# One core, a hybrid decoder layer: in its attention the loads of the next two heads are issued behind the second of eight query blocks instead of the fourth

## The chip, the core and the metric

The kernel runs on one core of a Trainium2 chip. It computes one decoder layer for 1024 tokens of width 1024 in float32. The metric is the device time of one execution in microseconds (us). Engines are called as in the profile: PE multiplies matrices, DVE works on vectors, ACT does activation functions, POOL simple work, and SP issues DMAs. SP's queue (SPq) is in order: a DMA whose semaphore wait is not met holds back every DMA behind it.

## The reference

Only the attention half of the layer matters here. Each query keeps the 256 keys with the highest indexer score; the kernel does that with an additive mask per query block, so that every query block of 128 rows meets all its causal keys. `setup_inputs` draws the inputs at random.

```python
def dsa_attention(q, k, v, iq, ik, iw):        # 8 heads of 64, 1024 tokens
    def block(i):                              # 128 queries
        ...
        _, idx = lax.top_k(score, topk)
        valid = idx <= qpos[None, :, None]
        ks = k[bidx, idx]
        vs = v[bidx, idx]
        s = jnp.einsum('bqhd,bqkhd->bhqk', qb, ks).astype(jnp.float32) * scale
        s = jnp.where(valid[:, None], s, -jnp.inf)
        p = jax.nn.softmax(s, axis=-1).astype(v.dtype)
        return jnp.einsum('bhqk,bqkhd->bqhd', p, vs)

def reference(...):
    proj = x @ w_in[l]                         # q, k, v, indexer and HGRN2 columns
    ...
    mix = jnp.concatenate([att, hgo], axis=-1) @ w_o[l]
    x = layer_norm(ALPHA * x + mix, ln1_g[l], ln1_b[l])
    h = jnp.square(jax.nn.relu(x @ w_up[l])) @ w_down[l]
    x = layer_norm(ALPHA * x + h, ln2_g[l], ln2_b[l])
```

## The kernel before

The kernel goes through the layer in stages: the input projection with the indexer's scores, the search for the 256th score and the HGRN2 heads beside it (to about 464 us), the attention (464 to 622 us), the output product with `w_o` and the first layer norm, the up product, the down product. Earlier stages have written the turned queries to DRAM as `qd`, the turned keys as `kd` and the values as `vd`; the additive masks lie on the core as `score` and `causal`.

The attention takes the eight heads in four pairs, hp = 0 to 3. For a pair `fetch` (line 658) issues seven DMAs on SP: two for the queries `qs` and four for the keys (two for each of the two `ks` tiles, one tile a head), each of 512 KB, and one for the values `va`, 512 KB too. In the rows below pair 1 and pair 3 have tiles of their own for queries and values (`qs1`, `va1`), which some views print as `qs` and `va` also; pairs 0 and 2 share one tile each. The `ks` tiles come from a ring of five buffers. Within `fetch` the first key DMA is told to wait for an instruction of ACT (`behind`, line 669): the last exp that had been written down before the call.

For each of the eight query blocks t of a pair, `scores(hp, t)` (line 674) makes on PE the products of the queries with the keys of both heads (lines 691 and 692, a bank of four at a time), moves them on DVE through the mask with a running maximum (line 693), negates the maximum on POOL (line 695), and takes the exp on ACT (line 697). `turn` (line 701) then transposes the exps on PE (line 710) into one of two banks, which DVE and ACT copy out as `pt` (lines 719 and 717); `gather` (line 722) multiplies them with the values two turns later (lines 733 to 738). `normalise` (line 748) has four products at line 751. The query blocks stand in the order t = 0, 1, 4, 5, 2, 3, 6, 7, and the turns of one group of two blocks stand behind the scores of the next group. So the scores of the next pair's blocks 0 and 1 come while blocks 6 and 7 of the pair before are still to be turned and gathered; this place is called the switch to a pair below.

The loop of line 770 walks through that plan and counts the calls of `scores` in `ns`. Pair 1 is fetched at ns = 4 of pair 0, in any case. Pairs 2 and 3 are fetched behind the block whose number is `FT`:

```python
            if (ns == 4 or ns > 8 and u[0] == FT) and hp < 3:
                fetch(hp + 1, pairs[hp]["last"])
```

FT is 5, which is the fourth block in the order above. Tiles and semaphore waits are set by the framework, which also simulates the program to set the order on each engine; where it puts the DMAs on SP is shown with the change.

Of the kernel before, what the change touches and what calls it, by code (L numbers as in the profile page):

```python
# [42 lines left out]
def layer(ctx, tc, x, w_in, w_o, lb_logits, hg_norm_g, ln1_g, ln1_b, w_up, w_down, ln2_g, ln2_b,  # L43
# [608 lines left out]
    bp = es_b.enter_context(tc.tile_pool(name="bp", bufs=1, reuse_waits="tile"))  # L652
    scale = HD ** -0.5
    PB = 5, 4
    PT, LAG, FT = 8, 2, 5
    pairs, probs, parts = {}, {}, {}

    def fetch(hp, after=None):
# [507 lines left out]
```

## Time and profile before

| what | value |
|---|---|
| median of 3 runs | 1389.93 us (1387.81 to 1395.92) |
| the profiled execution, its own time | 1392.06 us |
| its span, first to last instruction | 1390.3 us |
| PE busy | 1313.0 us, 94% of the span |
| DVE, ACT, POOL busy | 70%, 43%, 27% |
| mean granted clock of PE | 0.977 of full speed |
| PE idle for keys, line 691 | 7.4 us in three waits |

The profile is of one execution. The 1.8 us between its time and its span lie outside the instructions. A busy engine is not by that the one that sets the end; the chain of work that ended last and the idle time in front of PE's instructions say where time is lost. Everything that the change touches lies between 505 and 612 us.

### The profile page before, as it was taken

The page shows a single profiled execution, that of the slowest core. Times are in us where ns is not written, and L with a number is a line of the kernel's source. Part 1 is how long each engine was busy: PE and PEld are TensorE (multiplying, and loading weights), DVE is VectorE, ACT ScalarE, POOL GpSimd, SP SyncE. Part 2 cuts the span into 40 slices and gives each one's busy share as a digit, 9 for nine tenths or more (in the row PEclk, how much of TensorE's full clock was granted, in tenths as well). Part 3 has the DMA queues.
Part 4 walks back from the last instruction along what each step waited for, and adds up shares of the span by engine and source line. Part 5 has one row for each costly group of instructions (what it writes and reads, how often), then busy time and mean ns, then how long its engine had stood idle before and what let it go on. Part 6 is the DMA issues. An engine that isn't in the chain of part 4 may idle for free.

```text
span 1390.3 us, 20796 instructions
## 1 busy us (share of the span) xinstructions
PE 1313.0 (94%) x7961; PEld 1068.8 (77%) x7961; DVE 968.8 (70%) x1821; ACT 595.2 (43%) x1038; POOL 371.1 (27%) x344
## 2 busy tenths in 40 slices
PE   8999799789899999999998999999998899999996
PEld 8877678677679956667887888888886688888875
DVE  4556999999993445552278755666536999887568
ACT  3433346555422545552135555555545343333131
POOL 3433312534524201122472000000003432341016
PEclk9999999999999999999999999999999999999998
DMA  5333322101103364306422444444466554442123
GB/s 218 108 101 104 99 59 61 47 18 33 47 32 92 88 125 107 76 16 187 131 106 83 160 159 167 135 145 144 159 212 234 197 186 157 156 159 91 57 96 121
DMA packets 96948, 162.50 MB, mean 117 GB/s; under 512 B 5832, under 2 KB 41040, under 8 KB 96720
## 3 DMA queue, kind: packets, MB, share of 16 engines
q1 hardware_dynamic: 81584, 133.37, 31.0%
q10 hardware_dynamic: 15264, 27.79, 5.7%
q8 instruction: 63, 1.03, 0.3%
q14 instruction: 37, 0.30, 0.1%
HBM read 114.48 MB, written 46.66 MB: 116 GB/s over the span
## 4 chain that ended last, share of the span: by engine, by line
PE 63%; DVE 18%; DMA 8%; POOL 4%; issue 3%; ACT 3%; SPq 1%; POOLq 0%; DVEq 0%; ACTq 0%
PE ps L124 18%; PE ps L123 18%; PE ps L125 18%; DVE junk L313 5%; PE ps L736 3%; DMA ks<-kd 2%; DMA wraw<-in_w_in_dram 2%; PE ps L710 2%; DMA qd<-rparts 1%; DVE hgk L500 1%; POOL tn L911 1%; PE ps L691 1%; DVE hgq L499 1%; POOL acc L837 1%; DMA kd<-rparts 1%
## 5 line engine op out<-in xcount | busy, mean ns | idle before, releaser
L123 PE MATMUL ps<-tw,sh 128*128 128x512 f32 x392 | 153.9, 396 | 8.9 <-ACT tw L88 5.1
L123 PE MATMUL ps<-w,xt 128*128 128x512 f32 (+2 forms) x448 | 157.4, 356 | 2.3 <-ACT hgf L443 1.1
L125 PE MATMUL ps<-w,xt 128*128 128x512 f32 (+2 forms) x448 | 158.4, 355 | 0.0
L124 PE MATMUL ps<-w,xt 128*128 128x512 f32 (+2 forms) x448 | 157.9, 354 | 0.0
L124 PE MATMUL ps<-tw,sh 128*128 128x512 f32 x392 | 154.0, 393 | 1.0 <-DVE tw L89 1.0
L125 PE MATMUL ps<-tw,sh 128*128 128x512 f32 x392 | 152.5, 392 | 1.4 <-DVE sh L89 1.4
L89 POOL TENSOR_TENSOR w<-wraw,w 128x1024 fp32r<-128x1024 f32 (+2 forms) x46 | 95.5, 2086 | 117.8 <-ACT w L88 114.4
L1052 POOL TENSOR_TENSOR tt<-rb,rb 128x1536 f32<-128x1536 f32 (+1 forms) x5 | 19.4, 3873 | 392.9 <-DVE tw L89 327.0
L1074 DVE TENSOR_TENSOR acc<-acc,ps 128x512 f32<-128x512 f32 x140 | 92.1, 679 | 35.8 <-PE ps L125 35.6
L88 ACT ACTIVATE sh<-rs 128x1536 fp32r<-128x1536 f32 (+1 forms) x35 | 49.1, 1403 | 151.2 <-PE ps L125 141.1
L123 PE MATMUL ps<-xt,w 128*128 128x512 f32 x256 | 103.5, 404 | 0.0
L124 PE MATMUL ps<-xt,w 128*128 128x512 f32 x256 | 102.5, 400 | 0.0
L125 PE MATMUL ps<-xt,w 128*128 128x512 f32 x256 | 102.5, 401 | 0.0
L313 DVE TENSOR_SCALAR_CACHE_REDUCE junk<-score,cand 128x384 uint8<-128x384 f32 (+1 forms) x124 | 100.4, 810 | 2.7
L124 PE MATMUL ps<-xt,wq 128*128 128x512 f32 x256 | 99.9, 390 | 0.0
L123 PE MATMUL ps<-xt,wq 128*128 128x512 f32 x256 | 99.7, 389 | 0.0
L125 PE MATMUL ps<-xt,wq 128*128 128x512 f32 x256 | 99.5, 390 | 0.0
L345 ACT ACTIVATE sjunk<-score,scand 128x896 int8<-128x896 f32 (+1 forms) x62 | 67.9, 1095 | 67.7 <-DVE scand L355 49.8
L123 PEld LDWEIGHTS ps<-w,xt 128*128 128x128 f32 x448 | 85.7, 192 | 14.3 <-ACT hgf L443 1.5
L123 PEld LDWEIGHTS ps<-tw,sh 128*128 128x128 f32 x392 | 74.7, 191 | 25.8 <-ACT tw L88 5.5
L124 PEld LDWEIGHTS ps<-w,xt 128*128 128x128 f32 x448 | 85.5, 191 | 11.3 <-issue 0.8
L125 PEld LDWEIGHTS ps<-w,xt 128*128 128x128 f32 x448 | 85.6, 191 | 10.1
(240 smaller groups left out, 3081.4 us busy)
## 6 DMA issues: line engine op xcount, KB each, us to landing
hs<-h ACTq DMA_DIRECT2D x98, 256.0 KB
rs<-hs SPq DMA_DIRECT2D x28, 768.0 KB
wr<-in_w_up_dram SPq DMA_DIRECT2D x16, 1024.0 KB
rb<-in_w_down_dram SPq DMA_DIRECT2D x16, 768.0 KB
wraw<-in_w_in_dram SPq DMA_DIRECT2D x20, 512.0 KB
ks<-kd SPq DMA_DIRECT2D x16, 512.0 KB
xn<-in_x_dram SPq DMA_DIRECT2D x8, 512.0 KB
kd<-rparts SPq DMA_DIRECT2D x16, 256.0 KB
```

What stands on the lines that cost most here:

```text
L88: first = ACT.activation(hi, src, AF.Copy)
L89: (eng or DVE).tensor_tensor(lo, src, hi.bitcast(F32), op=OP.subtract)
L123: PE.matmul(ps, ah, bh, start=first, stop=False, **kw)
L124: PE.matmul(ps, ah, bl, start=False, stop=False, **kw)
L125: PE.matmul(ps, al, bh, start=False, stop=last, **kw)
L313: DVE.tensor_scalar(junk[:, :wide[j]], score[j], at, 0.0, op0=op, op1=OP.add, accum_out=res)
L345: ACT.activation(sjunk[:, :wide[NB + j]], score[NB + j], AF.Sign, bias=0.0 if bias is None else bias[:, j:j + 1], scale=1.0, accum_out=cnt ...
L499: DVE.tensor_tensor(qv[:, :, 1, :], qv[:, :, 1, :], t2[:, :, 0:1].to_broadcast([P, nb, m]), op=OP.mult)
L710: PE.transpose(tp[:, g % 2, i], probs[hp, 2 * m + i][hh][:, g * P:(g + 1) * P], ident)
L736: PE.matmul(o[sl, i:i + 2], lhs, pt[hh][:, g], start=c == 0 and g == 0, stop=c == m)
L1052: POOL.tensor_tensor(t1, b12, b11, op=OP.subtract)
L1074: DVE.tensor_tensor(acc[t][:, gs], acc[t][:, gs], ps, op=OP.add)
```

## The change

One number in line 655 is changed.

```diff
-    PT, LAG, FT = 8, 2, 5
+    PT, LAG, FT = 8, 2, 1
```

With it `fetch` for pairs 2 and 3 is called behind block t = 1 of the pair before, the second block, and the exp that its first key DMA waits for is that of block 1 instead of that of block 5. `fetch` itself, what it loads, the tiles and their number are the same. Pairs 0 and 1 are fetched as before.

On SP, the piece from the queries of pair 2 to the first weights of the next stage is this (`qs`, `va` without a number are the tiles of pair 2, those with a number the tiles of pair 3; x4 is four rows alike):

```order
 L49 DMA qs<-qd 64x2x1024 x2
+L49 DMA ks<-kd 64x2x1024 x4
 L49 DMA va<-vd 128x8x128
+L49 DMA qs_5806<-qd 64x2x1024 x2
 L49 DMA ks<-kd 64x2x1024 x4
-L49 DMA qs_5898<-qd 64x2x1024 x2
-L49 DMA va_5907<-vd 128x8x128
-L49 DMA ks<-kd 64x2x1024 x4
+L49 DMA va_5815<-vd 128x8x128
 L49 DMA wraw<-in_w_o_dram 128x2x512 x5
```

In both pairs the four key DMAs have moved ahead of the value DMA of their own pair; the queries still come first.

What the DMAs of pair 2 wait for on SP, with the change (DMAHW names are earlier DMAs, Activation is ACT):

```order
L49 DMA qs<-qd 64x2x1024 [waits DMAHW0_49,PE_49]
L49 DMA qs<-qd 64x2x1024 [waits DMAHW1_49]
L49 DMA ks<-kd 64x2x1024 [waits DMAHW2_49,Activation_49]
L49 DMA ks<-kd 64x2x1024 [waits DMAHW3_49]
L49 DMA ks<-kd 64x2x1024 [waits DMAHW4_49]
L49 DMA ks<-kd 64x2x1024 [waits DMAHW5_49]
L49 DMA va<-vd 128x8x128 [waits DMAHW6_49,PE_49]
```

The wait for ACT is now that for the exp of block 1 of pair 1, and the value DMA, which waits for PE to be done with the values of pair 0 in the same tile, no longer stands in front of the keys.

On PE, at the switch to pair 2, the rows with the change stand in the same order as before, and only the names of the DMAs that they wait for are others:

```order
 L691 MATMUL ps<-ks,qs_5200 128x512 [waits DVE_49]
 L692 MATMUL ps<-ks,qs_5200 128x512
-L691 MATMUL ps<-ks,qs 128x128 [waits DMAHW3_49,DMAHW1_49,DMAHW4_49,DMAHW0_49,DVE_49]
+L691 MATMUL ps<-ks,qs 128x128 [waits DMAHW2_49,DMAHW1_49,DMAHW3_49,DMAHW0_49,DVE_49]
 L692 MATMUL ps<-ks,qs 128x128
 L710 MATMUL ps<-ident,prs 128x128 [waits Activation_49]
 L710 MATMUL ps<-ident,prs 128x128 x3
-L691 MATMUL ps<-ks,qs 128x128 [waits DMAHW6_49,DMAHW5_49,DVE_49]
+L691 MATMUL ps<-ks,qs 128x128 [waits DMAHW5_49,DMAHW4_49,DVE_49]
 L692 MATMUL ps<-ks,qs 128x128
 L691 MATMUL ps<-ks,qs 128x256 [waits DVE_49]
```

Nothing has moved there; the two rows that wait for DMAs are the scores of block 0 with the keys of the pair's first and second head. On DVE, ACT and POOL no row is different.

## Rows read from the trace of the kernel before

**Rows 1.** The page: span; busy time by engine; the ended-last chain's shares by line.

```profile
span 1390.3 us, 20796 instructions
...
PE 1313.0 (94%) x7961; PEld 1068.8 (77%) x7961; DVE 968.8 (70%) x1821; ACT 595.2 (43%) x1038; POOL 371.1 (27%) x344
...
PE ps L124 18%; PE ps L123 18%; PE ps L125 18%; DVE junk L313 5%; PE ps L736 3%; DMA ks<-kd 2%; DMA wraw<-in_w_in_dram 2%; PE ps L710 2%; DMA qd<-rparts 1%; DVE hgk L500 1%; POOL tn L911 1%; PE ps L691 1%; DVE hgq L499 1%; POOL acc L837 1%; DMA kd<-rparts 1%
```

**Rows 2.** Waits, 455 to 645 us: waiter, releaser: us in total, times, longest.

```profile
PE ps L691 <- DMA ks<-kd: 7.4, 3, 3.3
```

**Rows 3.** PE's timeline, three switches: start, us, instruction, count [idle before <-releaser].

```profile
505.17 0.44 PE L691 MATMUL ps<-ks,qs 128*128 128x128 f32 x1 [3.31 <-DMA ks<-kd]
...
538.15 0.62 PE L710 MATMUL ps<-ident,prs 128*128 128x128 f32 x4
541.37 0.30 PE L691 MATMUL ps<-ks,qs 128*128 128x128 f32 x1 [2.60 <-DMA ks<-kd]
...
576.56 0.62 PE L710 MATMUL ps<-ident,prs 128*128 128x128 f32 x4
578.62 0.30 PE L691 MATMUL ps<-ks,qs 128*128 128x128 f32 x1 [1.44 <-DMA ks<-kd]
```

**Rows 4.** PE's timeline, the same work behind the second and third switch.

```profile
544.23 3.28 PE L736 MATMUL ps<-pt,va 128*64 128x256 f32 x21
...
550.82 0.60 PE L710 MATMUL ps<-ident,pr 128*128 128x128 f32 x4
...
580.64 2.59 PE L736 MATMUL ps<-pt,va 128*64 128x256 f32 x21
...
586.53 0.60 PE L710 MATMUL ps<-ident,pr 128*128 128x128 f32 x4
```

**Rows 5.** Stretches: us, busy PE PEld DVE ACT POOL; PEclk, DMA share, GB/s.

```profile
508.00:510.00 2.00, 2.00 (x7) 0.86 (x8) 0.98 (x7) 1.28 (x5) 0.21 (x1) 0.50 0.00 0
...
512.00:526.00 14.00, 14.00 (x88) 8.77 (x86) 6.50 (x21) 4.56 (x10) 1.04 (x3) 1.00 0.00 0
...
542.00:544.00 2.00, 2.00 (x9) 0.96 (x7) 0.54 (x4) 2.00 (x4) 1.08 (x2) 0.56 1.05 217
544.00:546.00 2.00, 2.00 (x12) 1.10 (x12) 1.03 (x4) 0.29 (x2) 0.38 (x1) 0.58 0.13 25
...
580.00:582.00 2.00, 2.00 (x19) 1.24 (x19) 1.05 (x4) 2.00 (x4) 1.51 (x2) 1.00 0.00 0
```

**Rows 6.** SP's timeline: start, us of issuing, DMA, count.

```profile
526.10 0.37 SPq L49 DMA_DIRECT2D va<-vd  x1
527.99 2.52 SPq L49 DMA_DIRECT2D ks<-kd  x4
...
566.41 2.52 SPq L49 DMA_DIRECT2D ks<-kd  x4
```

**Rows 7.** ACT's timeline: ends of the exps of three blocks.

```profile
510.18 0.19 ACT L697 ACTIVATION_READ_ACCUMULATOR prs<-prs,nm 128x1 f32 x1
...
544.10 0.19 ACT L697 ACTIVATION_READ_ACCUMULATOR pr<-pr,nm 128x1 f32 x1
...
550.60 0.19 ACT L697 ACTIVATION_READ_ACCUMULATOR prs<-prs,nm 128x1 f32 x1
```

**Rows 8.** PE's timeline: the two line-751 groups of pair 1 and of pair 3.

```profile
522.99 1.05 PE L751 MATMUL ps<-ident,wide 128*128 128x128 f32 x8
...
536.15 1.08 PE L751 MATMUL ps<-ident,wide 128*128 128x128 f32 x8
...
597.10 1.05 PE L751 MATMUL ps<-ident,wide 128*128 128x128 f32 x8
...
610.27 1.08 PE L751 MATMUL ps<-ident,wide 128*128 128x128 f32 x8
```

**Rows 9.** PE's timeline behind pair 3, where no next pair follows.

```profile
612.10 0.65 PE L710 MATMUL ps<-ident,prs 128*128 128x128 f32 x4
613.23 0.55 PE L710 MATMUL ps<-ident,prs 128*128 128x128 f32 x3 [0.47 <-DVE pt L719]
```

## The prediction

> **What bounds the kernel now.** I read the page first. PE is busy for 94% of the span, and in the chain of work that ended last the products at lines 123 to 125 come first; but one transfer of the attention stands in it too, the keys `ks` from `kd`, with 2% of the span [rows 1]. That chain has PE in the attention nearly all the time, so what counts there is where PE stands idle. The list of waits between 455 and 645 us names it: PE, at line 691, waited three times for the key transfer, 7.4 us in all, at most 3.3 [rows 2]. PE's own timeline puts the three pauses at the switches to pairs 1, 2 and 3: 3.31 us before 505.17, 2.60 us before 541.37, and 1.44 us before 578.62; the last two come right behind four transposes [rows 3]. The pause at pair 1 belongs to a fetch that the change leaves alone. So the change can work on 2.60 + 1.44 = 4.04 us of pauses, and on what they drag along.
>
> They do drag something along. From the end of the second pause at 541.37 to the transposes at 550.82 PE took 9.45 us; the same instructions behind the third switch, 578.62 to 586.53, took 7.91 us, and 21 products inside took 3.28 us against 2.59 [rows 3, 4]. The granted clock tells why: 0.56 and 0.58 in the two stretches from 542 to 546, where it was part of the time at the lower of its two levels (1.2 instead of 2.4 GHz), and 1.00 behind the third switch [rows 5]. PE had been idle for 2.60 us before the fall and for 1.44 us where none came. So the second pause cost 1.54 us more than its own length.
>
> **The change part by part.** What it moves is one call of `fetch` in pair 1 and one in pair 2, seven DMAs each, all on SP; it adds and removes no instruction, and no row moves on PE, DVE, ACT or POOL.
>
> The keys of pair 2. The first of the four key DMAs left SP at 527.99 [rows 6], and PE went on with the second head's keys at 541.37, 13.38 us later. With the change they wait for the exp of block 1, which ended at 510.18 + 0.19 = 510.37 [rows 7]; the queries stand ahead of them and wait only for pair 0's scores. The DMA engines moved nothing from 512 to 526 [rows 5], so there is room. With the old 13.38 us the keys lie on the core at 523.75. PE wants them when its four transposes before the pause end, 538.15 + 0.62 = 538.77 [rows 3]: 15.0 us to spare. The pause of 2.60 goes, and with it the reason that I see for the low clock: 2.60 + 1.54 = 4.14 us.
>
> The keys of pair 3. They left at 566.41 and PE went on at 578.62, 12.21 us later [rows 3, 6]. With the change they wait for the exp of block 1 of pair 2, which ended at 550.79 [rows 7] and will end 4.14 earlier, at 546.65; by the longer of the two transfers they are there at 560.03, and PE wants them at 577.18 - 4.14 = 573.04. The pause of 1.44 us goes. No fall of the clock followed it, so nothing is added.
>
> The queues passed. On SP the keys move ahead of the values. The value DMA of pair 2 left at 526.10 [rows 6], when PE's last products with pair 0's values were done, and that wait is the same: it leaves then in either case, with the keys no longer behind it. Behind it stand pair 3's queries, which wait for the end of pair 1's scores anyway, and behind pair 3's values the first weights of `w_o`, which wait for POOL. I count nothing for these. A key transfer that runs beside other work is another matter, as it now lies beside blocks 4 and 5. PE's work from one group of line 751 to the next took 536.15 - 522.99 = 13.16 us in pair 1, most of it beside the key transfer, and 610.27 - 597.10 = 13.17 us in pair 3, after the last one had landed [rows 8]. So a transfer beside it costs PE nothing.
>
> What is late next. Behind the two scores PE goes to the next transposes, which need a bank that DVE empties. The trace has a switch without keys: behind pair 3 no pair follows, and there PE waited 0.47 us for DVE's copy [rows 9]. At the real switches four short products stand in between, so I take 0, and keep 0.47 for each as the other end. Further on come the transposes of block 7, whose exp ended at 544.10 + 0.19 = 544.29 [rows 7]; they began at 550.82 and would begin at 546.68, so 2.39 us remain. ACT does those exps out of scores that PE has finished before the pause, so they don't wait for the new keys.
>
> The sum: 2.60 + 1.54 + 1.44 = 5.58 us. The lower end is 4.04 - 0.94 = 3.10, if the clock falls all the same and DVE's copy is waited for twice; I see no row for more than 5.58. Behind the attention the order on every engine is as before and each wait is for work that also comes earlier, so the gain reaches the end. Against the profiled execution: 1392.06 - 5.58 = 1386.5 (span 1384.7). That execution was 2.13 us above the median of the three runs; against the median it is 1389.93 - 5.58 = **1384.4 us**, 0.40% less.
>
> **The rivals.**
> - The clock falls anyway. Then only the pauses go: 4.04 us, 1385.9. For it: the low stretch lies on a piece with many transposes. Against it: the 14 us from 512 to 526 hold transposes too, and PE had 1.00 there, as it had behind the third switch [rows 5]. The Trainium skill, page "TensorE: Matmul & The Clock Gate", section "Part 4: PE-mode transpose", says that the full clock does not engage for transposes, as they don't count as busy in the same way; by that the low clock would be no matter of the pause and would stay, which is this rival. The two stretches just named speak against it.
> - Another wait takes the pause's place: DVE's copy, 0.47 us at either switch, with or without the clock. That gives 1389.93 - 5.58 + 0.94 = 1385.3, or 1386.8 with the low clock.
> - It doesn't do what it says: the keys still leave late, because something in front of them on SP holds them. Then nothing changes, 1389.9. The key DMA would have to leave 15 us later than I put it. Against it: with the values gone from in front, only the exp and landed transfers are waited for.
> - Slower. PE now runs ahead and comes to the transposes of blocks 6 and 7 before their exps, at lines 710 and 697; it pauses there, and the clock falls behind that pause. Priced by the first switch, 3.31 us of pause [rows 3], which had the clock at 0.50 [rows 5], and with the 1.54 us of the second for it: 4.85 us a switch, 9.70 for both, less the 5.58 gained: 4.1 us slower, 1394.1. It decides from a pause of about 1.3 us a switch (1.3 + 1.54 is half of 5.58), for which the exps would have to come 2.39 + 1.3 = 3.7 us later than they do. Nothing in the change delays them.
>
> **How the numbers follow.** Forecast 0.77, clock falls anyway 0.08, other wait 0.07, no effect 0.04, slower 0.04. A measurement of this kernel can tell about 0.5% from no change, here 6.95 us: faster by more means below 1382.98. The forecast lies 1.4 us above that line, and the three runs lie between 2.1 below and 6.0 above their median, so a median of a few runs can move by about 2 us: I give the forecast 0.3 to be seen below the line, 0.77 x 0.3 = 0.23 for faster. Slower by over 0.5% needs above 1396.9, which the slower rival's 1394.1 reaches only if its pauses are longer: 0.03. Within 0.5%: 0.74. The range takes 4 us below the forecast for the runs and goes up to where only no effect and slower are left out: 1380.5 to 1389.0.
>
> **What would show it.** Right: in the list of waits PE waits for `ks` once, some 3.3 us at pair 1, and no more; SP issues the keys of pair 2 near 510.4 and those of pair 3 near 546.7; PE begins the scores of pair 2 near 538.8 and of pair 3 near 573.0 without a pause; the granted clock is 1.00 in the 4 us behind both; the output product begins 5.6 us earlier. Wrong: a clock under 0.9 there without a pause (the first rival), a pause of PE for DVE or ACT within 8 us behind a switch (the second or the last), or key DMAs that still leave near 528 (the third). If all of this is right and the time is still the old one, the gain was given back behind the attention, which nothing here foresees.

## The result and the profile after

The changed kernel takes 1383.44 us (median of 13 runs, 1380.33 to 1386.0), the kernel before 1391.52 us beside it (13 runs, 1385.14 to 1396.61). The ratio is 0.995, with a 95% interval of 0.9937 to 0.9962: by the ratio 7.0 us less, between 5.3 and 8.8 (the two medians lie 8.08 us apart). A second timing of the same kernel gave 0.9945 (0.9921 to 0.9969). The forecast was 1384.4 us, 5.58 us less.

The profiled execution of after took 1383.45 us, that of before 1392.06. The head of its page answers to [rows 1]:

```profile
span 1381.7 us, 20797 instructions
...
PE 1310.3 (95%) x7961; PEld 1067.1 (77%) x7961; DVE 968.9 (70%) x1821; ACT 594.3 (43%) x1038; POOL 371.4 (27%) x344
```

The engines do the work of before, and PE is 2.7 us shorter busy. The span is 8.6 us shorter, so most of it is idle time of PE that is gone. The list of waits of after, 455 to 640 us (waiter, releaser: us in total, times, longest), has one wait for keys instead of three [rows 2]:

```profile
PE ps L691 <- DMA ks<-kd: 2.9, 1, 2.9
```

That one is at the switch to pair 1, which the change leaves alone (3.31 before, 2.85 here). SP's timeline of after (start, us of issuing, DMA, count) answers to [rows 6]:

```profile
509.01 2.52 SPq L49 DMA_DIRECT2D ks<-kd  x4
524.50 0.37 SPq L49 DMA_DIRECT2D va<-vd  x1
...
544.93 2.52 SPq L49 DMA_DIRECT2D ks<-kd  x4
558.64 0.36 SPq L49 DMA_DIRECT2D va<-vd  x1
```

The keys leave 19.0 us earlier for pair 2 and 21.5 us earlier for pair 3; the values, which wait for PE to be done with the old ones, leave 1.6 and 5.9 us earlier, as PE is. PE's timeline of after at the two switches (start, us, instruction, count [idle before <-releaser]) answers to [rows 3, 4], and its last three lines to [rows 9] and to the first product with `w_o`:

```profile
536.55 0.62 PE L710 MATMUL ps<-ident,prs 128*128 128x128 f32 x4
536.93 0.30 PE L691 MATMUL ps<-ks,qs 128*128 128x128 f32 x1
...
539.04 2.59 PE L736 MATMUL ps<-pt,va 128*64 128x256 f32 x21
...
544.94 0.60 PE L710 MATMUL ps<-ident,pr 128*128 128x128 f32 x4
...
555.52 0.72 PE L751 MATMUL ps<-ident,wide 128*128 128x128 f32 x5
...
570.68 0.62 PE L710 MATMUL ps<-ident,prs 128*128 128x128 f32 x4
571.06 0.31 PE L691 MATMUL ps<-ks,qs 128*128 128x128 f32 x1
...
573.18 2.59 PE L736 MATMUL ps<-pt,va 128*64 128x256 f32 x21
...
579.08 0.60 PE L710 MATMUL ps<-ident,pr 128*128 128x128 f32 x4
...
605.79 0.55 PE L710 MATMUL ps<-ident,prs 128*128 128x128 f32 x3 [0.48 <-DVE pt L719]
...
614.20 0.96 PE L123 MATMUL ps<-w,xt 128*128 128x512 f32 x3
```

Both switches now read alike: the second head's scores begin 0.38 us after the four transposes began, with no bracket behind them, and the 21 products take 2.59 us at either. The windows of after (columns as in [rows 5]) show the clock behind them, and the key transfers of pair 2 (first line) and pair 3 (546 to 556 us) beside blocks 4 and 5:

```profile
512.00:520.00 8.00, 8.00 (x50) 4.30 (x50) 2.63 (x7) 1.79 (x3) 0.00 (x0) 1.00 1.02 210
...
538.00:540.00 2.00, 2.00 (x16) 1.16 (x17) 1.74 (x10) 2.00 (x5) 0.43 (x2) 1.00 0.95 238
540.00:542.00 2.00, 2.00 (x23) 1.50 (x20) 0.36 (x2) 2.00 (x4) 1.29 (x1) 1.00 1.05 215
...
546.00:556.00 10.00, 10.00 (x60) 5.94 (x58) 4.18 (x13) 2.65 (x6) 0.21 (x1) 1.00 0.96 209
...
570.00:582.00 12.00, 12.00 (x87) 8.75 (x86) 6.62 (x25) 8.71 (x22) 2.62 (x6) 1.00 0.01 2
```

The DMA engines move some 210 GB/s from 512 to 520 us, where they moved nothing before [rows 5], PE is busy all through it, and the clock is 1.00 behind both switches.

### The profile page after: what moved, and what is told of

Its sections match the earlier page's. It is cut to its first block, busy times and chain, and to the rows that moved or that the text cites. A ratio compares the mean times of both kernels' runs of the same rounds, so it can differ in the third digit from the quotient of the medians.

```text
span 1381.7 us, 20797 instructions
## 1 busy us (share of the span) xinstructions
PE 1310.3 (95%) x7961; PEld 1067.1 (77%) x7961; DVE 968.9 (70%) x1821; ACT 594.3 (43%) x1038; POOL 371.4 (27%) x344
## 5 line engine op out<-in xcount | busy, mean ns | idle before, releaser
L125 PEld LDWEIGHTS ps<-w,xt 128*128 128x128 f32 x448 | 86.1, 192 | 10.4
```

The costliest lines, as they stand in the source:

```text
L125: PE.matmul(ps, al, bh, start=False, stop=last, **kw)
```

## One account for all traces

To compare executions I use four lengths from PE's timeline. **Attention** runs from the first product of line 691 to the first of `w_o`. **Pause** is the time from the start of the four transposes to the second head's scores, less the 0.38 us that stand there without a wait; it is 0.24 us more than the idle time in the bracket, which counts from the modelled end of the transposes. **Clock** is the time from the second head's scores to the next group of line 751, less 18.59 us. In after these are 555.52 - 536.93 = 18.59; in the twelve switches of all runs that had no pause and no reordered work they are 18.58 to 18.60. **Lost** is pauses and clock of the second and third switch together. The attention of before, 156.97 us, lies between these two lines of PE's timeline:

```profile
464.66 0.22 PE L691 MATMUL ps<-ks,qs 128*128 128x128 f32 x1
...
621.63 1.20 PE L123 MATMUL ps<-w,xt 128*128 128x512 f32 x4
```

That of after, 150.47 us, lies between this line and the one at 614.20 above:

```profile
463.73 0.22 PE L691 MATMUL ps<-ks,qs 128*128 128x128 f32 x1
```

All in us:

| kernel, one execution each | attention | pause + clock, switch 2 | pause + clock, switch 3 | lost |
|---|---|---|---|---|
| before | 156.97 | 2.84 + 1.44 | 1.68 - 0.11 | 5.9 |
| before, second trace (b_again) | 159.70 | 3.93 + 2.95 | 1.99 + 1.53 | 10.4 |
| before, third trace (b_same) | 159.24 | 3.83 + 2.67 | 2.71 + 1.42 | 10.6 |
| after | 150.47 | 0 | 0 | 0 |
| after, second trace (r_after) | 150.76 | 0 | 0 | 0 |
| e1_pair2 | 154.88 | 0 | 2.17 + 1.40 | 3.6 |
| e2_pair3 | 153.99 | 2.55 + 1.48 | 0 | 4.0 |
| e3_order | 157.01 | 2.92 - 0.10 | 2.95 + 2.90 | 8.7 |
| e6_ft4, r_ft4 | 150.89, 151.15 | 0 | 0 | 0 |
| e8_values | 156.89 | 2.59 + 2.88 | 2.06 + 1.47 | 9.0 |
| e8_again | 158.19 | 2.55 + 1.49 | 1.93 + 1.48 | 7.5 |
| e5_pair1 | 145.03 | 0 | 0 | 0 |

What else differs in the attention lies at the first switch, where PE paused 1.8 to 4.5 us in every trace but that of e5_pair1: from the first group of line 751 to the first product with `w_o`, less what is lost, all traces have 92.78 to 92.83 us, so the table leaves nothing out. The pauses are for keys, but for the third switch of e8_again, where the trace names DVE as the one that came last.

## Experiments

### One pair at a time

Pair 2's keys alone early:

```diff
-            if (ns == 4 or ns > 8 and u[0] == FT) and hp < 3:
+            if (ns == 4 or ns > 8 and u[0] == (1 if hp == 1 else FT)) and hp < 3:
```

> Only the fetch of pair 2 is moved behind block 1; pair 3 is fetched behind block 5 as before. Theory (each switch loses its own pause, and the second one also its half-clock stretch): PE's pause before pair 2 is gone, the one before pair 3 stays at about 1.4 us; in the trace the work up to the first scores of pair 3 comes 4.1 to 4.3 us earlier against the same kernel before (2.6 to 2.84 of pause, 1.44 to 1.54 of clock), time about 4.2 us less, ratio 0.997. Rival (the gain comes from the keys standing ahead of the values on SP and the transfers spreading out, so that one moved pair pulls the other along): the pause before pair 3 shrinks too and the ratio is near 0.995.

Measured: 1387.32 us, ratio 0.9963 (0.995 to 0.9976), 5.1 us less. Pair 3's keys alone early:

```diff
-            if (ns == 4 or ns > 8 and u[0] == FT) and hp < 3:
+            if (ns == 4 or ns > 8 and u[0] == (1 if hp == 2 else FT)) and hp < 3:
```

> Only the fetch of pair 3 is moved behind block 1; pair 2 is fetched behind block 5 as before. Theory: the pause before pair 2 stays at about 2.6 us with the low clock behind it, the one before pair 3 is gone; 1.4 to 1.7 us less, ratio 0.9988. Rival (the low clock behind pair 2's pause is not bound to that pause, or pair 3's fall is seen in other executions): more than 3 us less with this part alone, ratio under 0.998.

Measured: 1386.93 us, ratio 0.9969 (0.9956 to 0.9981), 4.3 us less. PE's timeline of e1_pair2, the second and the third switch:

```profile
539.14 0.62 PE L710 MATMUL ps<-ident,prs 128*128 128x128 f32 x4
539.51 0.31 PE L691 MATMUL ps<-ks,qs 128*128 128x128 f32 x1
...
575.82 0.32 PE L691 MATMUL ps<-ks,qs 128*128 128x128 f32 x1 [1.93 <-DMA ks<-kd]
```

and of e2_pair3:

```profile
534.27 0.30 PE L691 MATMUL ps<-ks,qs 128*128 128x128 f32 x1 [2.31 <-DMA ks<-kd]
...
569.88 0.30 PE L691 MATMUL ps<-ks,qs 128*128 128x128 f32 x1
```

Each half takes away the pause of its own switch and leaves the other, and each is worth half of the gain or somewhat more: 5.1 and 4.3 us add up to 9.4 where both together gave 7.0, which the intervals allow. Pair 3's half brings more than its pause of 1.44 us in [rows 3], as the rival in its expectation said. The table says why: with a pause left at the third switch e1_pair2 lost 1.40 us to the clock there, which the profiled execution of before had not.

### How much the kernel before loses, from one execution to the next

The kernel before was traced twice more, first beside the runs of the next section, later timed against itself.

> The kernel before, profiled once more, to see how its pauses differ from one execution to the next. Theory (the loss at pair 3's switch was small by chance in the first profile): pauses of 2 to 3 us at both switches, and 1.4 to 3 us of clock behind at least one. Rival (the pauses are fixed by the order and repeat): again 2.6 and 1.4 us, with a clock fall behind the first of the two alone.

> The kernel before, timed against itself, for what a comparison of this size shows where nothing differs. Theory (the comparisons are even): a ratio whose interval holds 1, within 0.997 to 1.003, and an attention of 157 to 160 us with pauses of 2 to 4 us at the switches to pairs 2 and 3. Rival (the kernel that is named second is favoured, or executions differ by more than the intervals say): a ratio of 0.996 to 0.998 with an interval below 1, as the versions with the keys' order or the values changed have shown without a shorter attention in their traces; then about 0.3% has to come off every gain.

Measured: against itself 1391.85 us, ratio 1.0003 (0.9988 to 1.0018), so a kernel measured against itself comes out even. PE's timeline of b_again, the second heads' scores at the second and third switch:

```profile
535.26 0.45 PE L691 MATMUL ps<-ks,qs 128*128 128x128 f32 x1 [3.69 <-DMA ks<-kd]
...
574.35 0.30 PE L691 MATMUL ps<-ks,qs 128*128 128x128 f32 x1 [1.75 <-DMA ks<-kd]
```

and of b_same:

```profile
541.62 0.44 PE L691 MATMUL ps<-ks,qs 128*128 128x128 f32 x1 [3.59 <-DMA ks<-kd]
...
581.13 0.30 PE L691 MATMUL ps<-ks,qs 128*128 128x128 f32 x1 [2.46 <-DMA ks<-kd]
```

Both have longer pauses than [rows 3] at both switches, and both lost to the clock at both. Windows of b_same, 3 to 6 us behind the second and the third switch (columns as in [rows 5]), show the clock still low behind the second and back behind the third:

```profile
545.00:547.00 2.00, 2.00 (x10) 1.01 (x10) 0.99 (x4) 0.00 (x0) 0.41 (x1) 0.50 0.00 0
...
585.00:587.00 2.00, 2.00 (x21) 1.24 (x19) 0.62 (x2) 1.16 (x6) 0.00 (x0) 0.97 0.00 0
```

The loss comes in three sizes. Of the 14 pauses at these two switches in all traces, two had none behind them, eight 1.40 to 1.53 us and four 2.67 to 2.95 us; the granted clock in the 6 us behind the pause was 1.00, 0.72 and 0.50. The three traces lose 5.9, 10.4 and 10.6 us there, 9.0 in the mean. The execution that the forecast was made from is the smallest of the three; the timed gain of 5.3 to 8.8 us lies between.

### Is the place, or the queue order, what counts?

With FT = 4 the fetches stand behind the third block; the keys have less room, and there is no switch where they come late: in r_ft4 pair 2's keys left SP at 525.42, and PE took them at 539.43, 14.01 us later, without a wait. The changed kernel ran once more beside it.

```diff
-    PT, LAG, FT = 8, 2, 5
+    PT, LAG, FT = 8, 2, 4
```

> Half the move: pairs 2 and 3 are fetched behind block 4, the third in the order, so the keys wait for its exp, which ends near 524.5 on the old scale, 3.5 us earlier than block 5's and 14 us later than block 1's; the keys stand ahead of the values. Theory (any arrival before PE wants the keys is as good as any other): keys there near 535.5 to 538, wanted at 538.8, so no pause at either switch, and the same time as with block 1: ratio 0.995 to 0.996. Rival (the earlier the better, through something else than the pause): clearly less gain than block 1, ratio 0.998.

> The changed kernel again, beside the third block's version on one chip. Theory (a key transfer that is there in time is as good as an earlier one; the pauses and the clock falls that they bring are all of the gain): ratio 0.994 to 0.996, in the trace no pause at the switches to pairs 2 and 3, 18.6 us from either switch to the next group of line 751, and 149 to 151 us from the first scores to the first output product. Rival (block 1 is too early and loses about 3 us against block 4 somewhere): its ratio stays 0.002 to 0.003 above that of the third block's version.

> Fetch behind the third block (t = 4) again, beside the changed kernel. Theory: the same time as the changed kernel within 0.2%, so the lead of its first measurement was chance. Rival: 0.2% to 0.3% less than the changed kernel once more.

Measured: e6_ft4 1380.37 us, ratio 0.9923 (0.9906 to 0.994). That looked better than after, so both ran side by side: r_ft4 1382.52 us, 0.994 (0.992 to 0.996), r_after 1383.69 us, 0.9945 (0.9921 to 0.9969). They are the same, and the traces agree: no pause at either switch, attentions of 150.5 to 151.2 us. Once the keys are in time, how early they are is worth nothing.

The change also moves the keys ahead of the values on SP. e3_order does that alone: the fetch stays behind block 5, and for pairs 2 and 3 the value DMA is told to wait for the exp as the keys are, and is issued behind them.

```diff
-        dma(va, vd[:, hp * P:(hp + 1) * P].rearrange("(t p) n -> p t n", p=P))
+        behind(dma(va, vd[:, hp * P:(hp + 1) * P].rearrange("(t p) n -> p t n", p=P)), after) if hp > 1 else dma(va, vd[:, hp * P:(hp + 1) * P].rearrange("(t p) n -> p t n", p=P))
```

> The calls stay behind block 5, but the value DMA of pairs 2 and 3 is made to wait for the same exp as the keys, which puts it behind the four key DMAs on SP: the order part of the change without the earlier issue. Before, the values (512 KB) left 1.9 us ahead of the keys and went beside them. Theory (the keys' arrival sets PE's pause): 512 KB at the 220 GB/s of that stretch are 2.4 us that the keys no longer share, so pair 2's pause shrinks from 2.6 to 0.2 to 1.0 us and no low clock follows, pair 3's 1.44 us to nothing; 3 to 5 us less, ratio 0.9965 to 0.998. Rival (the transfer's length is set by the keys alone, or by their issue): the pauses stay at 2.6 and 1.4 us, ratio 1.000; then only the earlier issue counted.

Measured: 1388.62 us, ratio 0.9981 (0.9966 to 0.9995). SP's timeline of e3_order:

```profile
519.13 2.52 SPq L49 DMA_DIRECT2D ks<-kd  x4
521.76 0.53 SPq L49 DMA_DIRECT2D va<-vd  x1
...
556.11 2.53 SPq L49 DMA_DIRECT2D ks<-kd  x4
```

PE's timeline of it:

```profile
532.61 0.30 PE L691 MATMUL ps<-ks,qs 128*128 128x128 f32 x1 [2.68 <-DMA ks<-kd]
...
569.59 0.45 PE L691 MATMUL ps<-ks,qs 128*128 128x128 f32 x1 [2.70 <-DMA ks<-kd]
```

and its windows behind the two pauses:

```profile
532.00:536.00 4.00, 3.39 (x26) 2.27 (x28) 1.57 (x8) 3.66 (x8) 1.46 (x2) 1.00 1.10 230
...
569.00:573.00 4.00, 3.41 (x12) 2.25 (x12) 0.60 (x4) 3.41 (x7) 1.08 (x2) 0.53 0.14 34
```

The queue order alone leaves the pauses: 2.68 and 2.70 us, with 13.48 us from the first key DMA to PE at both. The same two pauses had two ends: behind the first the clock stayed at 1.00, behind the second it was 0.53, and the work to the next group of line 751 took 18.49 and 21.49 us. A fall of the clock is thus likely behind such a pause, but not fixed by its length.

e8_values leaves the keys at block 5 and moves the values of both pairs behind block 7, so that pair 2's keys go out without values beside them. The value load becomes a function of its own:

```diff
-        va = bq.tile([P, NT, P], F32, name="va1") if hp % 2 else bp.tile([P, NT, P], F32, name="va")
-        dma(va, vd[:, hp * P:(hp + 1) * P].rearrange("(t p) n -> p t n", p=P))
-        pairs[hp] = {"ks": ks, "qs": qs, "va": va}
+        pairs[hp] = {"ks": ks, "qs": qs}; hp > 1 or values(hp)
+    def values(hp, after=None):
...
-            ns += 1
+            ns += 1; hp in (1, 2) and u[0] == 7 and values(hp + 1, pairs[hp]["last"])
```

> The kernel before (keys behind the fourth block), but the value DMAs of pairs 2 and 3 are moved to behind block 7, so that pair 2's four key DMAs go out with no values beside them; pair 3's keys stay behind the values of pair 2 on SP. Theory (the 512 KB of values that go out beside the keys lengthen the key transfer): pair 2's keys need about 11 us instead of 12.2 to 14.5 from the issue to PE's second head, so PE's pause at the switch to pair 2 falls to 0.5 us or less, the clock stays at 1.00 behind it, and the attention is about 2.5 to 5 us shorter than in before (156.97 and 159.70 us). Rival (the transfer takes as long alone, or the keys leave no earlier): the pause at that switch stays at 2.3 to 3.9 us, and only chance moves the time. Either way the switch to pair 3 keeps its pause of 1.4 us or more.

> The version with the values behind block 7 once more, since its time was lower by 1.3 to 5.8 per mille and its trace had an attention as long as before's. Theory (its attention is no shorter, the lower time is chance or bias): attention 156 to 160 us again, and a ratio that is the same as that of before against itself. Rival (its pauses vary, and the traced execution was one of its long ones): attention 151 to 155 us here, with a pause under 1 us or no fall of the clock at one switch.

Measured: e8_values 1386.89 us, ratio 0.9964 (0.9942 to 0.9987); e8_again 1388.76 us, 0.9981 (0.9964 to 0.9998). SP's timeline of e8_values:

```profile
522.69 2.52 SPq L49 DMA_DIRECT2D ks<-kd  x4
...
539.02 0.37 SPq L49 DMA_DIRECT2D va<-vd  x1
```

PE's timeline of it at the second switch:

```profile
535.81 0.45 PE L691 MATMUL ps<-ks,qs 128*128 128x128 f32 x1 [2.35 <-DMA ks<-kd]
```

and its windows:

```profile
524.00:533.00 9.00, 8.68 (x60) 6.84 (x59) 6.38 (x20) 4.78 (x13) 1.87 (x4) 1.00 1.04 223
533.00:534.00 1.00, 0.47 (x5) 0.23 (x3) 1.00 (x4) 0.43 (x1) 0.00 (x0) 1.00 0.50 94
```

The theory that the values lengthen the key transfer failed: with nothing beside it the transfer took 535.81 - 522.69 = 13.12 us to PE's start, and 13.09 in e8_again, where 11 were expected; with the values beside it, it took 13.38, 14.48 and 14.39 in the three traces of before and 13.09 in e2_pair3. My 11 us had mixed two measures. In after the traffic ends 11 us after the issue; in e8_values it does so as well (9 us at 223 GB/s and 1 us at 94 are the four times 512 KB), and PE starts some 2 us behind its end. The Trainium skill, page "DMA: Bandwidth & Descriptors", section "Anatomy of one DMA — SWDGE (gpsimd) path", puts some 2 us beside the moving of the data, most of it for the receipt of the last write; these DMAs are issued by SP, and the 2 us behind the end of the traffic agree with it in size. That they go to the receipt is shown by no run here.

Why e3_order and the two runs of e8 were 0.2 to 0.4% faster than before is open. Their traced attentions, 156.9 to 158.2 us, are like those of before, 157.0 to 159.7. An open difference of this size is nearly as large as the timed gain of each half in e1_pair2 and e2_pair3, so it is their traces that tell the halves apart and not their times alone.

### Does the clock fall because PE is idle?

e9_fill is the kernel before with twelve products of 128x512 on old tiles, in front of the second head's first scores at the second and third switch. Their result is not used, and all loads are those of before.

```diff
+    def fill(hp): ps, kp = mm_bank(), pairs[hp - 1]; [PE.matmul(ps, kp["qs"][:, 0, :P], kp["ks"][0][:, 0, :512], start=i == 0, stop=i == 11) for i in range(12)]
...
-                ps = mm_bank()
+                hp > 1 and t == 0 and hh and fill(hp); ps = mm_bank()
```

> The kernel before with twelve extra products of 128x512 for PE, some 3.6 us by 1.20 us for four at line 123, in front of the second head's first scores at the switches to pairs 2 and 3; their result is not used. They keep PE at work for the time in which it waited for keys; the loads are those of before. Theory (the clock falls because PE has been idle): the pause is gone or below 1.3 us, and the granted clock stays at 1.00 in the 4 us behind both switches. Rival (it falls for what stands there, transposes and short products, or because of the transfer): the clock behind one or both switches is under 0.9 all the same, without a pause of PE. The time itself says little, since the planner puts some other work into another order around the extra products.

Measured: one execution of 1386.76 us beside 1392.73 for before. PE's timeline of e9_fill at the second switch:

```profile
532.85 3.05 PE L657 MATMUL ps<-ks,qs 128*128 128x512 f32 x12
535.74 0.22 PE L691 MATMUL ps<-ks,qs 128*128 128x128 f32 x1
...
537.40 2.38 PE L736 MATMUL ps<-pt,va 128*64 128x256 f32 x20
```

and its windows behind the second and the third switch:

```profile
536.00:538.00 2.00, 2.00 (x15) 1.14 (x16) 0.52 (x4) 2.00 (x4) 1.47 (x2) 1.00 0.36 72
538.00:540.00 2.00, 2.00 (x24) 1.40 (x22) 0.75 (x3) 1.82 (x8) 0.00 (x0) 1.00 1.00 236
...
575.00:577.00 2.00, 2.00 (x24) 1.42 (x22) 0.73 (x3) 1.67 (x8) 0.00 (x0) 1.00 0.00 0
```

The keys were let go as in before (by SP at 522.32, 13.42 us ahead of the scores), the same transposes and short products stand behind the switch, in a slightly other order, and the clock stays at 1.00. So the fall comes with PE's idle time, not with what stands there and not with the transfer; this is one execution with two switches, beside the twelve switches without a pause, none of which had a fall. The extra products took 2.89 and 3.03 us of PE, and by the account above the two switches cost 5.7 us together, against 5.9, 10.4 and 10.6 in the traces of before: useless work in place of the wait cost no more than the wait, and in two of three cases much less.

### The switch that the change left

The keys of pair 1 can be sent early in the same way. e5_pair1 is the changed kernel with the key loads split from `fetch` into a function `load`; for pair 1 it is called behind the second block of pair 0.

```diff
+    def load(hp, after=None):
...
+        ks = keys.pop(hp, None) or load(hp, after)
...
-                next(g1)
+                next(g1); ns and keys.update({1: load(1, pairs[0]["last"])})
```

> On top of the changed kernel, the four key DMAs of pair 1, whose pause the change leaves alone, are issued behind block 1 of pair 0 instead of behind its fifth block; queries and values of pair 1 where they were. Theory (the same mechanism at the first switch): its keys leave about 480 instead of 490 us, the pause of 2.9 to 3.5 us at that switch is gone and with it the clock fall, which cost up to 3 us there; 3 to 6 us less than the changed kernel, ratio to before 0.990 to 0.993. Rival (at the first switch something else comes as late, the queries or DVE, or the transfer moved forward delays the first output weights or pair 1's queries, which now stand behind it): the pause stays under another name and the ratio is that of the changed kernel.

Measured: 1378.02 us (5 runs, 1377.56 to 1378.31), ratio 0.9909 (0.9881 to 0.9937); after beside it had 0.9945. SP's timeline of e5_pair1:

```profile
474.44 2.55 SPq L49 DMA_DIRECT2D ks<-kd  x4
```

and PE's at the first switch:

```profile
498.60 0.33 PE L691 MATMUL ps<-ks,qs 128*128 128x128 f32 x1
498.88 0.27 PE L691 MATMUL ps<-ks,qs 128*128 128x128 f32 x1
```

The keys leave at 474.44 instead of 489.41 in after, and PE goes from the first head to the second without a wait. The attention is 145.03 us, 5.7 less than in r_after, and the time 5.7 us less. This is the fastest version.

## Why the prediction was right, and which term was too small

**What bounds it.** Right. Three pauses for keys, of which two could go, went; e1_pair2 and e2_pair3 show each by itself.

**The pauses.** The keys were put at 510.4 and 546.7 on SP and left at 509.01 and 544.93. That is not the change: this execution reached the attention 0.93 us earlier and spent 0.68 us less from there to the first group of line 751 (521.38 - 463.73 us against 522.99 - 464.66, the first switch), 1.6 us together. The scores of the second heads began at 536.93 and 571.06, expected near 538.8 and 573.0, for the same reason and by the 0.24 us of the bracket. "I count nothing" for the queues held: the values left SP 15.5 and 13.7 us behind the keys and nobody waited for them.

**The clock.** Right in kind: 1.54 us were counted behind the second pause, 1.44 are there in the same execution. That it is idleness was an inference from two switches; e9_fill bears it out. The rival that the clock falls anyway is out: twelve switches without a pause took 18.58 to 18.60 us, whatever the transposes. The Trainium skill's page "TensorE: Matmul & The Clock Gate", section "Part 4: PE-mode transpose", says that transposes don't bring the full clock; stretches with many of them among other products ran at 1.00 here, in after and in e9_fill; a stretch of transposes alone was not measured.

**A transfer beside it costs PE nothing.** Right, and better shown now: the 18.59 us behind the second switch of after, 536.93 to 555.52, hold nearly all of pair 3's key transfer, 209 GB/s from 546 to 556 us, and the 18.60 us behind the third hold none.

**What is late next.** Right at 0: no bracket for DVE or ACT follows either switch, and the 0.48 us at the end of pair 3 was there before [rows 9]. The slower rival had no trace of its pause.

**The term that was mis-sized.** It is "The pause of 1.44 us goes. No fall of the clock followed it, so nothing is added", and with it "I see no row for more than 5.58". Between the two profiled executions the two switches give 4.28 + 1.57 = 5.85 us, close to 5.58 (the two brackets are short by 0.24 us each, and the clock gave 0.21 less). But the first trace of before was a mild one. Its third switch had cost 1.57 us; the two other traces of before paid 3.5 and 4.1 there, and e1_pair2 3.6. The clock fell behind 12 of the 14 pauses of all traces at these two switches. A forecast from three traces would have said 9.0 us; from one, 5.58; the timing says 5.3 to 8.8. The 5.58 lies inside that, so the ratio does not refute it; the other traces, and the 8.08 us between the medians, say that it was too small.

**Luck.** That the time came out within 1.0 us of 1384.4 is in part luck. The median of three runs that it started from, 1389.93, lay 1.59 us below the later one of thirteen, 1391.52, and the gain was put 2.50 us below the distance of the medians; the two errors have opposite signs.

**The rest of the 8.6 us** by which the two spans differ is not the change: 0.93 ahead of the attention, 0.68 at the first switch and some 1.2 behind the attention, beside the 5.85 of the two switches. So the first product with `w_o` began 7.43 us earlier, 614.20 for 621.63, where 5.6 were expected.

## What to carry to other kernels

Follow each wait of PE for a transfer to the instruction that lets the DMA go, and ask how much earlier that could be; once the data are in time, earlier still is worth nothing (FT = 1 and 4 are the same). Price a pause of PE with the clock behind it, and take both from several executions or from all like places of the trace, since pauses of 2.68 and 2.70 us here cost 0 and 2.9 us more. When a fix works at two of three like places, look at the third: here it was worth another 5.7 us.

## What the runs showed of the hardware

- Two pauses of 2.68 and 2.70 us in one execution (e3_order): no fall of the clock behind the first, 2.9 us lost behind the second. By the brackets, one of 1.69 us had a fall behind it (e8_again, third switch, 1.48 us lost), and that of 1.44 us in before had none.
- What the clock cost behind such a pause came in three sizes: none (2 of 14), 1.40 to 1.53 us (8), 2.67 to 2.95 us (4). The longer of two pauses did not always cost more: 1.44 us behind 2.60 (before), 2.88 behind 2.35 (e8_values).
- Four key DMAs of 512 KB took 12.2 to 14.5 us from the first issue to PE's start, and for pair 2 neither the values' place behind them in the queue (13.48) nor their absence (13.12 and 13.09) took it out of the range of what it was with the values ahead (13.09 to 14.48).
- The same code reached the attention at 458.6 to 466.5 us, so the spans of two traces differ by several microseconds ahead of anything that the change touches; lengths within the stage are what can be compared.
